# Small tables in two pools: where weights and activations start in SBUF

## The chip, the cores and the metric

The kernel runs on one core of a Trainium2 chip. The metric is the device time of one execution in microseconds (us), the median of three runs. A profile of one execution shows each engine: PE is the matrix engine (TensorE), PEld its weight loads, DVE the vector engine, ACT the scalar engine, POOL is GpSimd, SP the engine that issues most DMAs. SBUF is the on-chip memory: 128 partitions, in each of which a tile has the same byte address.

## The reference

A decoder trunk of two layers over 512 tokens of width 1024, in float32. Each layer has three steps, each followed by a residual sum and a layer norm:

```python
x = layer_norm(ALPHA * x + 0.5 * swiglu_ffn(x, ffn1_w_gu[l], ffn1_w_down[l]), ...)
x = layer_norm(ALPHA * x + hybrid_mixer(x, w_in[l], w_out[l], ...), ...)
x = layer_norm(ALPHA * x + 0.5 * swiglu_ffn(x, ffn2_w_gu[l], ffn2_w_down[l]), ...)

def swiglu_ffn(x, w_gu, w_down):
    a, u = jnp.split(x @ w_gu, 2, axis=-1)      # 1024 -> 2 * 2816
    return (jax.nn.silu(a) * u) @ w_down        # 2816 -> 1024
```

The mixer projects x once, runs windowed attention with sinks on half of the columns and retention with decay on the other half, normalises the retention per head, gates it, and projects back. Most of the work is the matrix products of the four feed-forward steps.

## The kernel before

**Products in three parts.** A float32 operand is split into a high part (rounded to fp32r) and a low part (the rest): `split` (L168 on ACT, L169 on DVE). `mm3` (L183 to L185) then issues three matmuls for each product: high by high, and the two mixed ones. A matmul has 128 columns of weights (the stationary operand, loaded just before by a weight load) and a moving operand of 256 or 512 columns, and adds into PSUM (`ps`). In the profile's names `ps<-xh,uh` the first after the arrow is the moving operand and the second the weights. Every matmul has a weight load of its own; the load for the next matmul starts as the current matmul starts.

**Units and raws.** Weights come from HBM by DMA into `raw` (two tiles of 8 KB a partition), and are split into a *unit*: a pair `uh`, `ul` of 128 x 1024 (4 KB a partition each). There are six such pairs (`UBUFS`). A unit holds eight blocks of 128 columns, 512 bytes each, or two blocks of 512 columns. `Weights` (L47 and below) hands the units out in a fixed order and starts the split of a new one when one is given back (`W.done`).

**The activations** lie transposed in `xh` and `xl` (128 x 8 x 512 each).

**One feed-forward step** (`ffn`). It goes through the gate and up columns in 11 groups of 256 columns. Groups 2 to 10 (`SEVEN`) use `glu7`, seven half-size products in place of eight: some multiply units by blocks of `xh`, `xl` (`xb`), the others by sums of such blocks held in `Th`, `Tl` (`tb`), all 256 columns wide. Groups 0 and 1 are plain (`glu`), 256 or 512 columns wide. The down projection (`seventh`, `down`) turns the operands round: activations, written block by block into `xh`, `xl` by `operand`, are the weights, and units are the moving operand, 512 columns wide. Its weight sums are made by DMAs on POOL's queue that add into `R` (L389). A few products of each down projection use other weights: `early` (a unit that holds activations) and `room` (`hr`).

**The mixer** multiplies units by `xh` (feature-major) and `xh` by units (token-major, `proj_tok`), both 512 or 256 wide. The output projection (`half`) uses `ya` with weights in the 4 KB tiles `b` of pool `mix`, then `xh` with units.

**Small tables.** `mhalf` is a constant of -0.5 for a power on POOL. Pool `small` holds statistics of the layer norm (`st`, `mv`, `ve`, `rs`), of the attention (`den`, `m`, `es`) and of the retention (`gmu`, `gvar`), three buffers each. `sk` and `nsk` hold the sinks.

**Where tiles lie.** Pools are laid out one behind the other in the order in which they are opened, and a tile takes its bytes rounded up to 32. 2,176 bytes (2,048 of DMA scratch and four constants of 32) come first. So in the kernel before:

| pool | what | bytes a partition | start of its main tiles, modulo 512 |
|---|---|---|---|
| base | `ident` 512, `mhalf` 32, `xh`, `xl`, `Y` 16,384 each | 49,696 | `ident` 128; `xh`, `xl`, `Y` 160 |
| rawp | 2 x 8,192 | 16,384 | `raw` 160 |
| unit | 12 x 4,096 | 49,152 | `uh`, `ul` 160 |
| small | `st` 3 x 64, eight others 3 x 32 | 960 | |
| ffn pools | `hT` 45,056, `S`, `Th`, `Tl` and others | | `hT`, `S`, `Th`, `Tl`, `R`, `hr` 96 |
| mixer pools | tables 6,144 with `rsc` 128 and `sk`, `nsk` 32 each beside them, then the rest | | `qk`, `rr`, `va`, `b`, `ya`, `vr` 288 |

The tables of the mixer's first row are `ropeC`, `ropeS`, `band`, `causal` and `diag`. The pools of a step start where `small` ends, and take one another's place from step to step.

Of the kernel before, what the change touches and what calls it, by code (L numbers as in the profile page):

```python
# [7 lines left out]
F32 = mybir.dt.float32  # L8
# [10 lines left out]
P = 128  # L19
# [27 lines left out]
class Weights:  # L47


    def __init__(self, T, items):  # L50
        self.T, self.items = T, items
        self.emitted = self.taken = self.out = 0
        self.ready = []
        self.raws = {}
        self.last = {raw: i for i, (raw, _, _, _) in enumerate(items)}
# [44 lines left out]
class Trunk:  # L100
    def __init__(self, tc, ctx):
        self.tc, self.nc = tc, tc.nc
        self.n = 0
        self.now = 0
        self.pin = True
        self.tasks = []
        self.later = []
        self.pace = None
        self.halves = 2
        nc = self.nc  # L110
        self.base = ctx.enter_context(tc.tile_pool(name="base", bufs=1))
        self.rawp = ctx.enter_context(tc.tile_pool(name="rawp", bufs=2))
        self.unit = ctx.enter_context(tc.tile_pool(name="unit", bufs=UBUFS))
        self.small = ctx.enter_context(tc.tile_pool(name="small", bufs=3))
        self.psum = ctx.enter_context(tc.tile_pool(name="psum", bufs=8, space=PSUM))
        self.ident = self.base.tile([P, P], F32, name="ident")
        make_identity(nc, self.ident)
        self.mhalf = self.base.tile([P, 8], F32, name="mhalf")
        nc.vector.memset(self.mhalf, -0.5)
        self.xh = self.base.tile([P, KC, SEQ], F32R, name="xh")  # L120
        self.xl = self.base.tile([P, KC, SEQ], F32R, name="xl")
        self.Y = self.base.tile([P, NT, D], F32, name="Y")
# [370 lines left out]
    def norm(self, t, halves, gb, out=None, delay=4, scale=(ALPHA, ALPHA)):  # L493
        nc = self.nc
        g, b = gb
        y = self.Y[:, t, :]
        st = self.small.tile([P, 2, 6], F32, tag="st", name=self.nm("st"))
        for h in range(2):
            hs = slice(h * 512, (h + 1) * 512)
            nc.vector.scalar_tensor_tensor(out=y[:, hs], in0=y[:, hs], scalar=scale[h], in1=halves[h],  # L500
                                           op0=ALU.mult, op1=ALU.add)
            nc.vector.bn_stats(out=st[:, h, :], in_=y[:, hs])
        mv = self.small.tile([P, 2], F32, tag="mv", name=self.nm("mv"))
        nc.vector.bn_aggr(out=mv, in_=st)
        ve = self.small.tile([P, 1], F32, tag="ve", name=self.nm("ve"))
        nc.vector.tensor_scalar_add(ve, mv[:, 1:2], LN_EPS)
        rs = self.small.tile([P, 1], F32, tag="rs", name=self.nm("rs"))
        nc.gpsimd.tensor_tensor(out=rs, in0=ve, in1=self.mhalf[:, 0:1], op=ALU.pow)
        nc.vector.scalar_tensor_tensor(out=y, in0=y, scalar=mv[:, 0:1], in1=g, op0=ALU.subtract, op1=ALU.mult)
        parts = [slice(0, D)] if out is None else [slice(0, 512), slice(512, D)]  # L510
        for hs in parts:
            nc.vector.scalar_tensor_tensor(out=y[:, hs], in0=y[:, hs], scalar=rs, in1=b[:, hs],
                                           op0=ALU.mult, op1=ALU.add)
            if out is not None:
                nc.sync.dma_start(out[t * P : (t + 1) * P, hs], y[:, hs])
        if out is None:
            self.pend.append(self.spawn(self.y_to_xT(t), delay))
# [293 lines left out]
    def mixer(self, sinks, cst, g, b):  # L811
        nc, tc, W = self.nc, self.tc, self.W
        with ExitStack() as ctx:
            cp = self.cpool = ctx.enter_context(tc.tile_pool(name=self.nm("mixc"), bufs=1))
            pool = self.mpool = ctx.enter_context(tc.tile_pool(name=self.nm("mix"), bufs=1))
            self.c = {}
            c = self.c

            def const(name, tag=None):
                ap = cst[name]  # L820
                c[name] = cp.tile(list(ap.shape), F32, tag=tag or name, name=self.nm(name))
                nc.sync.dma_start(c[name], ap)
# [2 lines left out]
            const("ropeS", "sin")  # L825
            for name in ("band", "causal", "diag", "rsc"):
                const(name)
            sk = c["sk"] = cp.tile([P, 8], F32, name=self.nm("sk"))
            nc.sync.dma_start(sk, sinks.partition_broadcast(P))
            c["nsk"] = cp.tile([P, 8], F32, name=self.nm("nsk"))  # L830
            nc.vector.tensor_scalar_mul(c["nsk"], sk, -1.0)

            self.kT = [self.tmp("qk", 6, F32R) for _ in range(2)]
# [128 lines left out]
    def attention(self, n):  # L962


        nc = self.nc
        c = self.c
        k0 = max(n - 1, 0) * P
        nk = (n + 1) * P - k0
        nb = nk // P
        ns = slice(n * P, (n + 1) * P)  # L970
        mm = nc.tensor.matmul
        s = [self.big([P, 4, 2 * P]) for _ in range(2)]
        for c2 in range(2):
            sb = [self.ps().rearrange("p (c k) -> p c k", c=2) for _ in range(2)]
            q, k = self.qT[c2], self.kT
            for cc in range(2):
                for i, (qi, ki) in enumerate(((0, 0), (0, 1), (1, 0))):
                    for kv in range(2):
                        pr = slice(kv * HD, (kv + 1) * HD)
                        mm(sb[kv][:, cc, :nk], q[qi][pr, cc, ns], k[ki][pr, k0 : k0 + nk], start=i == 0, stop=i == 2)  # L980
            for kv in range(2):
                nc.vector.tensor_tensor(out=s[kv][:, c2 * 2 : c2 * 2 + 2, :nk], in0=sb[kv][:, :, :nk],
                                        in1=c["band"][:, None, 2 * P - nk :].to_broadcast([P, 2, nk]), op=ALU.min)
        for kv in range(2):
            hs = slice(kv * 4, kv * 4 + 4)
            den = self.small.tile([P, 4], F32, tag="den", name=self.nm("den"))
            m = self.small.tile([P, 4], F32, tag="m", name=self.nm("m"))
            nc.vector.tensor_reduce(out=m, in_=s[kv][:, :, :nk], op=ALU.max, axis=AX.X)
            nc.vector.scalar_tensor_tensor(out=m, in0=m, scalar=-SCALE, in1=c["nsk"][:, hs], op0=ALU.mult, op1=ALU.min)
            es = self.small.tile([P, 4], F32, tag="es", name=self.nm("es"))  # L990
            nc.vector.tensor_add(es, m, c["sk"][:, hs])
            for cc in range(4):
                nc.scalar.activation(s[kv][:, cc, :nk], s[kv][:, cc, :nk], AF.Exp, bias=m[:, cc : cc + 1], scale=SCALE,
                                     accum_out=den[:, cc : cc + 1])
            nc.scalar.activation(es, es, AF.Exp)
            nc.vector.tensor_add(den, den, es)
            nc.vector.reciprocal(den, den)
            for cc in range(4):
                nc.scalar.activation(s[kv][:, cc, :nk], s[kv][:, cc, :nk], AF.Copy, scale=den[:, cc : cc + 1])
            yield 3  # L1000
        pT = []
        for kv in range(2):
            pT.append(self.big([P, 2, 512]))
            for kb in range(nb):
                tb = self.ps()
                for cc in range(4):
                    nc.tensor.transpose(tb[:, cc * P : (cc + 1) * P], s[kv][:, cc, kb * P : (kb + 1) * P], self.ident)  # L1007
                nc.scalar.copy(pT[kv][:, kb, :], tb)
            yield 1 + kv
        yb = self.ps()  # L1010
        for kb in range(nb):
            blk = n - nb + 1 + kb
            for kv in range(2):
                cs = slice(kv * HD, (kv + 1) * HD)
                mm(yb[cs, :], self.va[:, blk, cs], pT[kv][:, kb, :], start=kb == 0, stop=kb == nb - 1)  # L1015
        self.split(self.ya[0][:, :, ns], self.ya[1][:, :, ns], yb.rearrange("p (c q) -> p c q", c=4))

    def retention(self, p, qT, kT):
        nc = self.nc
        c, vr, O = self.c, self.vr, self.O  # L1020
# [9 lines left out]
        for h, sb in enumerate(banks):  # L1030
            st = self.tmp("rr", 10).rearrange("p (n i) -> p n i", n=NT)
# [19 lines left out]
        st = self.tmp("rr", 10)[:, :N3].rearrange("p (n e) -> p n e", n=NT - 1)  # L1051
# [19 lines left out]
        G = 2 * NT  # L1071
# [1 line left out]
        nc.vector.tensor_tensor(out=oc, in0=ob.rearrange("p (n h e) -> p n h e", n=NT, h=2),  # L1073
                                in1=wq[:, None, hp, None].to_broadcast([P, NT, 2, HD]), op=ALU.mult)
        ocg = oc.rearrange("p n h e -> p (n h) e")
        mu = self.small.tile([P, G], F32, tag="gmu", name=self.nm("gmu"))
        nc.vector.tensor_reduce(out=mu, in_=ocg, op=ALU.add, axis=AX.X)
        nc.vector.tensor_scalar_mul(mu, mu, 1.0 / HD)
        nc.vector.tensor_tensor(out=ocg, in0=ocg, in1=mu[:, :, None].to_broadcast([P, G, HD]), op=ALU.subtract)
# [108 lines left out]
```

## Time and profile before

| | |
|---|---|
| median of three runs | 1766.73 us (1766.64 to 1767.32) |
| span of the profiled execution | 1765.1 us, 1.6 us under the median |
| granted TensorE clock, mean | 0.998 of full speed |
| ACT casts L168 `uh<-S`, 128 x 1024 | 144, mean 1049 ns |
| DVE subtractions L169 `ul<-S,uh`, 128 x 1024 | 144, mean 1222 ns |
| DMA | 216.34 MB, mean 123 GB/s |

Busy time is the time in which at least one instruction of an engine runs, so two matmuls in flight count once. In the groups of instructions, the two numbers behind the count are the busy time in us and the mean duration of one in ns, and behind the second bar stands the idle time before them with what ended it. In the timeline, the first number is the start of an instruction in us from the start of the span, the second its duration. In the table of stretches, each engine has its busy time and, in brackets, the number of instructions, and the row ends with the granted clock, the busy share of the DMA engines and GB/s. In the view of waits a row has the total, the number and the longest.

### The profile page before, as it was taken

The numbers are of one execution on the slowest core, as the hardware profiler recorded it, in microseconds if no ns is written. First come the engines' busy times: TensorE is split into PE (matmuls) and PEld (weight loads), VectorE is DVE, ScalarE is ACT, GpSimd is POOL, SyncE is SP. The second block draws the span as 40 slices with busy tenths as digits, with TensorE's granted clock in tenths as the row PEclk, the third lists the DMA queues.
The fourth block names the chain that finished last, engine by engine and source line by source line (L and its number), as shares of the span: only waits on it lengthen the run. The fifth ranks groups of instructions, "written<-read, shape, count | busy, mean of one in ns | idle before, by whom it ended". The sixth has DMA issues, their size and how long they took to land.

```text
span 1765.1 us, 29166 instructions
## 1 busy us (share of the span) xinstructions
PE 1752.7 (99%) x11930; PEld 1600.5 (91%) x11930; DVE 1414.9 (80%) x1975; ACT 928.1 (53%) x1456; POOL 182.9 (10%) x152
## 2 busy tenths in 40 slices
PE   9999999999999999999999999999999999999998
PEld 9999988887789999998899999889877899999886
DVE  7888888856767888878888888888567587888887
ACT  5455556378712455555535555554795234555561
POOL 0000022111111000014000000311011110000131
PEclk9999999999999999999999999999999999999999
DMA  6234389422222243369423334982233122334891
GB/s 191 97 96 133 131 202 199 131 85 88 73 79 72 74 137 102 97 208 214 140 68 99 121 96 147 211 203 91 85 95 96 48 95 97 97 96 132 211 218 48
DMA packets 163765, 216.34 MB, mean 123 GB/s; under 512 B 5168, under 2 KB 116528, under 8 KB 163632
## 3 DMA queue, kind: packets, MB, share of 16 engines
q1 hardware_dynamic: 141872, 172.55, 30.5%
q0 software_dynamic: 21760, 41.95, 13.1%
q8 instruction: 93, 1.52, 0.3%
q14 instruction: 40, 0.33, 0.1%
HBM read 212.38 MB, written 2.10 MB: 122 GB/s over the span
## 4 chain that ended last, share of the span: by engine, by line
PE 90%; issue 6%; DMA 1%; DVE 1%; POOL 1%; ACT 0%; SPq 0%; POOLq 0%; DVEq 0%
PE ps L183 29%; PE ps L185 29%; PE ps L184 29%; PE ps L476 1%; DMA raw<-in_ffn_w_gu_dram 1%; POOL sw L959 1%; PE ps L1067 1%; PE ps L1015 0%; PE ps L1029 0%; PE ps L1063 0%; PE ps L1050 0%; DMA retS<-c_retS_dram 0%; ACT sw L957 0%; DVE ul L169 0%; PE ps L1007 0%
## 5 line engine op out<-in xcount | busy, mean ns | idle before, releaser
L183 PE MATMUL ps<-xh,uh 128*128 128x256 f32 (+1 forms) x1616 | 482.2, 298 | 0.0
L185 PE MATMUL ps<-xh,ul 128*128 128x256 f32 (+1 forms) x1616 | 479.3, 297 | 1.0 <-DVE ul L169 0.9
L184 PE MATMUL ps<-xl,uh 128*128 128x256 f32 (+1 forms) x1616 | 478.5, 296 | 0.3 <-DVE xl L169 0.3
L168 ACT CAST uh<-raw 128x1024 fp32r<-128x1024 f32 (+1 forms) x274 | 237.1, 886 | 245.6 <-PE ps L184 140.1
L169 DVE TENSOR_TENSOR ul<-raw,uh 128x1024 fp32r<-128x1024 f32 (+1 forms) x274 | 273.3, 1013 | 62.2 <-ACT uh L168 61.6
L183 PE MATMUL ps<-Th,uh 128*128 128x256 f32 x1152 | 319.1, 277 | 0.0
L184 PE MATMUL ps<-Tl,uh 128*128 128x256 f32 x1152 | 318.7, 277 | 0.0
L185 PE MATMUL ps<-Th,ul 128*128 128x256 f32 x1152 | 318.3, 276 | 0.0
L185 PEld LDWEIGHTS ps<-xh,ul 128*128 128x128 f32 x1616 | 307.9, 191 | 10.1 <-DVE ul L169 1.6
L183 PEld LDWEIGHTS ps<-xh,uh 128*128 128x128 f32 x1616 | 307.9, 191 | 9.7 <-issue 1.6
L184 PEld LDWEIGHTS ps<-xl,uh 128*128 128x128 f32 x1616 | 308.0, 191 | 7.9 <-DVE xl L169 0.5
L183 PE MATMUL ps<-uh,xh 128*128 128x512 f32 x720 | 283.4, 394 | 0.5 <-ACT xh L168 0.5
L185 PE MATMUL ps<-uh,xl 128*128 128x512 f32 x720 | 280.8, 390 | 0.0
L184 PE MATMUL ps<-ul,xh 128*128 128x512 f32 x720 | 280.3, 389 | 0.0
L168 ACT CAST uh<-S 128x1024 fp32r<-128x1024 f32 x144 | 151.1, 1049 | 149.0 <-PE ps L184 145.2
L169 DVE TENSOR_TENSOR ul<-S,uh 128x1024 fp32r<-128x1024 f32 x144 | 175.9, 1222 | 60.1 <-ACT uh L168 59.5
L184 PEld LDWEIGHTS ps<-Tl,uh 128*128 128x128 f32 x1152 | 216.7, 188 | 0.0
L183 PEld LDWEIGHTS ps<-Th,uh 128*128 128x128 f32 x1152 | 216.6, 188 | 0.0
L185 PEld LDWEIGHTS ps<-Th,ul 128*128 128x128 f32 x1152 | 216.4, 188 | 0.0
L389 POOL DMA_DIRECT2D R<-in_ffn_w_down_dram x80 | 97.1, 1217 | 1020.7 <-DVE ul L169 930.0
L169 DVE TENSOR_TENSOR ul<-R,uh 128x1024 fp32r<-128x1024 f32 x120 | 145.1, 1221 | 25.8 <-ACT uh L168 25.7
L183 PEld LDWEIGHTS ps<-uh,xh 128*128 128x128 f32 x720 | 135.2, 188 | 30.1 <-issue 1.6
(143 smaller groups left out, 2362.4 us busy)
## 6 DMA issues: line engine op xcount, KB each, us to landing
raw<-in_ffn_w_gu_dram SPq DMA_DIRECT2D x86, 1024.0 KB, 5.5
R<-in_ffn_w_down_dram POOLq DMA_DIRECT2D x80, 512.0 KB, 7.6
raw<-in_w_in_dram SPq DMA_DIRECT2D x18, 1024.0 KB, 5.2
R<-in_ffn_w_down_dram SPq DMA_DIRECT2D x16, 1024.0 KB, 6.3
raw<-in_ffn_w_down_dram SPq DMA_DIRECT2D x12, 1024.0 KB, 7.2
R<-in_ffn_w_down_dram SPq DMA_DIRECT2D x8, 512.0 KB, 4.3
raw<-in_w_in_dram SPq DMA_DIRECT2D x8, 512.0 KB, 6.1
raw<-in_w_out_dram SPq DMA_DIRECT2D x8, 512.0 KB, 6.4
```

The lines of the kernel that those rows point to most:

```text
L168: a = self.nc.scalar.copy(hi, src)
L169: b = self.low = self.nc.vector.tensor_sub(lo, src, hi.bitcast(F32))
L183: keep(mm(out, ah, bh, start=start, stop=False, **kw))
L184: keep(mm(out, ah, bl, start=False, stop=False, **kw))
L185: keep(mm(out, al, bh, start=False, stop=stop, **kw))
L389: self.nc.gpsimd.dma_start(src, rows(i, j, g * 2, 2), accum_op=ALU.add))
L476: nc.tensor.transpose(b[:, c * P : (c + 1) * P], src[:, c * P : (c + 1) * P], self.ident)
L959: nc.gpsimd.tensor_mul(sw[:, :n], sw[:, :n], S)
L1067: ins = nc.tensor.matmul(ob[:, o0 : o0 + HD], ST[h][:, n, :], vr[:, n, p * P + h * HD : p * P + (h + 1) * HD], start=n == 0, stop=n == 0 o ...
```

## The change

`mhalf` leaves pool `base` and goes, 16 columns wide, into a new pool `near` that is opened between `rawp` and `unit`. The tables `st`, `den`, `m`, `es` and `gmu` move from `small` to `near`, with three buffers as before. `mv`, `ve`, `rs` and `gvar` stay in `small`. `sk` and `nsk` get 16 columns, of which the first 8 are used. What is computed does not change, nor does the order of the work as it is written, but for the memset of `mhalf`, which now stands before the making of `ident`.

```diff
         self.rawp = ctx.enter_context(tc.tile_pool(name="rawp", bufs=2))
+        self.near = ctx.enter_context(tc.tile_pool(name="near", bufs=3))
+        self.mhalf = self.near.tile([P, 16], F32, tag="mhalf", name="mhalf", bufs=1)
+        nc.vector.memset(self.mhalf, -0.5)
         self.unit = ctx.enter_context(tc.tile_pool(name="unit", bufs=UBUFS))
         self.small = ctx.enter_context(tc.tile_pool(name="small", bufs=3))
...
-        self.mhalf = self.base.tile([P, 8], F32, name="mhalf")
-        nc.vector.memset(self.mhalf, -0.5)
...
-        st = self.small.tile([P, 2, 6], F32, tag="st", name=self.nm("st"))
+        st = self.near.tile([P, 2, 6], F32, tag="st", name=self.nm("st"))
...
-            sk = c["sk"] = cp.tile([P, 8], F32, name=self.nm("sk"))
+            sk = c["sk"] = cp.tile([P, 16], F32, name=self.nm("sk"))[:, :8]
...
-            c["nsk"] = cp.tile([P, 8], F32, name=self.nm("nsk"))
+            c["nsk"] = cp.tile([P, 16], F32, name=self.nm("nsk"))[:, :8]
...
-            den = self.small.tile([P, 4], F32, tag="den", name=self.nm("den"))
-            m = self.small.tile([P, 4], F32, tag="m", name=self.nm("m"))
+            den = self.near.tile([P, 4], F32, tag="den", name=self.nm("den"))
+            m = self.near.tile([P, 4], F32, tag="m", name=self.nm("m"))
...
-            es = self.small.tile([P, 4], F32, tag="es", name=self.nm("es"))
+            es = self.near.tile([P, 4], F32, tag="es", name=self.nm("es"))
...
-        mu = self.small.tile([P, G], F32, tag="gmu", name=self.nm("gmu"))
+        mu = self.near.tile([P, G], F32, tag="gmu", name=self.nm("gmu"))
```

## The prediction

> **What bounds the kernel now.** I read the page's first part, then the chain that ended last, then the waits of PE.
>
> ```profile
> span 1765.1 us, 29166 instructions
> PE 1752.7 (99%) x11930; PEld 1600.5 (91%) x11930; DVE 1414.9 (80%) x1975; ACT 928.1 (53%) x1456; POOL 182.9 (10%) x152
> PE 90%; issue 6%; DMA 1%; DVE 1%; POOL 1%; ACT 0%; SPq 0%; POOLq 0%; DVEq 0%
> ```
> ```profile
> PE ps L468 <- POOL ident masks.py:199: 1.4, 1, 1.4
> PE ps L185 <- DVE ul L169: 0.9, 2, 0.7
> PE ps L1029 <- DVE rr L1032: 0.8, 2, 0.4
> ```
> The matrix engine is busy 99% of the span and its longest waits for others come to some 3 us. So the time is the number of matmuls times the pace at which one follows another. Only something that changes that pace moves the time, and all of such a change counts until a producer is late.
>
> The mean duration of a matmul is not its pace, because two are in flight at once. The pace is read from start times. First, products of xh with units, 256 columns wide: 48 of them, from 57.37 to the start of the first product with Th.
>
> ```profile
> 57.37 0.28 PE L183 MATMUL ps<-xh,uh 128*128 128x256 f32 x1
> ...
> 63.00 0.28 PE L185 MATMUL ps<-xh,ul 128*128 128x256 f32 x1
> 63.12 0.29 PE L183 MATMUL ps<-Th,uh 128*128 128x256 f32 x1
> ```
> That is 5.75 us / 48 = 119.8 ns. Next the 60 products with Th from 63.12, of the same shape and with the same kind of unit as weights, up to the next product with xh (the last of the 60 and that one):
>
> ```profile
> 69.82 0.28 PE L185 MATMUL ps<-Th,ul 128*128 128x256 f32 x1
> 69.94 0.28 PE L183 MATMUL ps<-xh,uh 128*128 128x256 f32 x1
> ```
> 6.82 us / 60 = 113.7 ns. Then 179 starts of the 512-column products in the down projection:
>
> ```profile
> 249.62 0.39 PE L184 MATMUL ps<-ul,xh 128*128 128x512 f32 x1
> ...
> 289.96 0.39 PE L185 MATMUL ps<-uh,xl 128*128 128x512 f32 x1
> ```
> 40.34 us / 178 = 226.6 ns. The difference between 512 and 256 columns, 226.6 - 119.8 = 106.8 ns, is the streaming of 256 columns. What is left over is an **overhead per matmul**: 13.0 ns for xh at either width, 6.9 ns for Th.
>
> Why should Th be cheaper? By the layout given with the kernel, units and xh both start 160 bytes past a multiple of 512, and Th 96 past one. Every block of weights is 128 columns = 512 bytes and every moving block 1024 or 2048, so these remainders hold for all blocks. **Distance 0 costs 13.0 ns, distance 64 costs 6.9 ns.** The weight loads say the same, being a little longer with xh:
>
> ```profile
> L183 PEld LDWEIGHTS ps<-xh,uh 128*128 128x128 f32 x1616 | 307.9, 191 | 9.7 <-issue 1.6
> L183 PEld LDWEIGHTS ps<-Th,uh 128*128 128x128 f32 x1152 | 216.6, 188 | 0.0
> ```
> I take it that the load of the next weights and the running stream read SBUF at once, and hinder each other when they start at the same remainder. That is inferred from two distances, not shown.
>
> **The change part by part.** The instructions, their number, their buffers and their DMAs stay. Two tables per layer get 32 bytes wider; SyncE issues the same loads. The memset of mhalf takes 16 columns instead of 8:
>
> ```profile
> L119 DVE MEMSET mhalf<- 128x8 f32 x1 | 0.1, 65 | 0.8 <-PEq L1174 0.8
> ```
> 65 ns at the start, under the wait of 1.4 us for ident: nothing.
>
> What changes are remainders. Without mhalf in base, xh, xl, Y and raw go from 160 to 128. The pool near holds 64 + 192 + 3*96 + 96 = 640 bytes, so units start at (128 + 640) mod 512 = 256. Pool small holds 4*96 = 384, so hT and Th start at (256 + 384) mod 512 = 128. In the mixer 128 + 128 + 64 + 64 = 384 for ya and the t4k tiles, both alike as before. So the distance from activation to unit becomes 128, for xh and for Th. Where the unit is the moving operand and xh the weights (down products, token-major projections), it is -128. Counts:
>
> ```profile
> L183 PE MATMUL ps<-xh,uh 128*128 128x256 f32 x1408 | 398.5, 283 | 0.0
> L183 PE MATMUL ps<-Th,uh 128*128 128x256 f32 x1152 | 319.1, 277 | 0.0
> L183 PE MATMUL ps<-uh,xh 128*128 128x512 f32 x720 | 283.4, 394 | 0.5 <-ACT xh L168 0.5
> L183 PE MATMUL ps<-xh,uh 128*128 128x512 f32 x208 | 83.6, 402 | 0.0
> ```
> Each stands for three (L183 to L185): 4224 with xh at 256 columns, 3456 with Th, and 3 * (720 + 208) = 2784 at 512. The 480 with hr, yah or another unit as weights keep distance 0.
>
> No row shows distance 128. One end: it helps no more than 64 does, 6.9 ns. The other is the least overhead in the trace, 16 transposes in 1.91 us:
>
> ```profile
> 895.84 1.91 PE L476 MATMUL ps<-ident,Y 128*128 128x128 f32 x16
> L476 PE MATMUL ps<-ident,Y 128*128 128x128 f32 x192 | 25.2, 276 | 0.3 <-DMA Y<-in_x_dram 0.3
> ```
> (1.91 - 0.28) / 15 = 108.7 to 109.3 ns by rounding; I use 109.3, so 2.5 ns over 106.8. A straight line through 13.0 and 6.9 would be below that at 128. I take the middle, **4.7 ns**, for both signs:
> - xh, 256 columns: (13.0 - 4.7) * 4224 = 35.1 us
> - Th: (6.9 - 4.7) * 3456 = 7.6 us
> - 512 columns: (13.0 - 4.7) * 2784 = 23.1 us
>
> Together 65.8 us. With 6.9 ns it is 25.8 + 0 + 17.0 = 42.8 us; with 2.5 ns 44.4 + 15.2 + 29.2 = 88.8 us.
>
> The Trainium skill, "TensorE: Matmul & The Clock Gate", section "Back-to-back issue gap", gives N/2.4 + 2.5 ns for matmuls in a row, so 109.2 and 215.8 ns here. No product of this trace reaches that; by it the sum would be the 88.8 us end.
>
> **What it costs.** Transposes of Y have ident 32 bytes away now and 0 after: at most the 6.1 ns between Th and xh on 192 of them, 1.2 us; I take 0.5. Then the cover: does a faster PE catch up with its producers?
>
> ```profile
> 82.60:102.20 19.60, 19.60 (x171) 19.60 (x170) 16.98 (x27) 10.62 (x16) 0.00 (x0) 1.00 0.33 108
> 233.10:314.70 81.60, 81.60 (x363) 67.55 (x362) 70.99 (x70) 47.06 (x49) 24.39 (x20) 1.00 0.99 219
> ```
> ```profile
> ACT uh L168 <- PE ps L184: 294.9, 263, 4.2
> DVE ul L169 <- ACT uh L168: 148.9, 181, 4.7
> ACT uh L168 <- DMA R<-in_ffn_w_down_dram: 37.7, 35, 2.4
> ```
> One group of gate products takes 19.6 us, with 16.98 us of DVE. Even the full gain of 10% there leaves DVE some slack, and ACT mostly waits for PE to give units back, not the other way round. The down projection is tighter: in its 81.6 us DVE works 71.0 and the DMA engines are full, and ACT already waits for R. There 360 products would save 8.3 ns each, 3.0 us of 81.6. Six units lie ready ahead, 12 matmuls of 226.6 ns each, so 2.7 us a unit; that swallows 3 us. If it didn't, the four stages would give back 12 us at most. I take 2 us lost, mixer included, where chains of DVE, ACT and POOL are short of cover.
>
> 65.8 - 0.5 - 2 = 63.3 us. The profiled execution is 1765.1 us of span, 1.6 under the median of 1766.7; that rest stays. **1766.7 - 63.3 = 1703.4, said as 1704 us.**
>
> **The rivals.**
> 1. Nothing beyond Th's pace: any distance but 0 costs 6.9 ns. For it: a weight load reads 512 bytes while the stream reads 1024, so the one may overtake the other once wherever they start. 42.8 - 2.5 = 40.3 us, 1726.
> 2. The hindrance goes altogether, 2.5 ns left: 88.8 - 4 = 85 us, 1682; producers cost more then.
> 3. The sign counts: -128 does nothing for the 512-column products. All of those with a distance that I can see are at 0, so nothing speaks against it. 35.1 + 7.6 - 2.5 = 40 us, 1727; with Th's pace for xh only 25.8 us, 1741.
> 4. **Slower**: what counts is the distance modulo 128, not 512. Then 128 is as bad as 0, xh gains nothing, and Th, which has 64 by chance, loses it: 3456 * 6.1 = 21.1 us, 1788. It decides as soon as the other 7008 products gain under 21.1 / 7008 = 3.0 ns each. Neither 0 nor 64 tells a period of 128 from one of 512.
> 5. Nothing happens: xh and Th differ by where they lie (xh ahead of the units, Th behind them), or the remainders are not what I worked out. 1766.7. Against it: the 13.0 ns is the same at both widths and with either operand as weights.
>
> The Trainium skill has a rule for the fifth: in "TensorE: Matmul & The Clock Gate", section "Step-by-step: what each phase is for", "Loading the next tile's weights doesn't steal SBUF read bandwidth from the running matmul". By that rule start addresses cannot matter. The trace does not agree as it stands: 119.8 against 113.7 ns for one shape, so it gets little.
>
> **How the numbers follow.** Forecast, overhead between 3.5 and 6 ns: 0.34. Rival 1: 0.20, rival 2: 0.18, rival 3: 0.14, rival 4: 0.09, rival 5: 0.05. Faster by over 0.2% (3.5 us, about what a measurement of this kernel can tell): 0.86; same 0.05; slower 0.09. The range takes the forecast and rivals 1 to 3, from 1676 (rival 2 with nothing lost is 1678) to 1742; rivals 4 and 5 stay out.
>
> **What would show it.** Right: 48 products with xh at under 5.5 us instead of 5.75; their weight loads at 188 ns or less instead of 191; the mean duration of a 512-column product with xh below 394 ns; PE still at 99%. The step on distance 128 is wrong if xh keeps 119.8 or Th slows to it; the step on signs if 512 columns stay at 226.6; the cover if PE's waits for ACT uh or DVE ul grow beyond 5 us. A product with hr or yah should keep 227; if it changes as well, remainders are not the reason.

## The result: slower by 1.5%, and the profile after

The changed kernel takes 1793.99 us (median of 4 runs, 1793.76 to 1794.6), the kernel before on the same chip 1767.03 us (4 runs, 1766.64 to 1767.98). The ratio is 1.0153, with a 95% interval of 1.0138 to 1.0167: 27.0 us slower, where 63 us of gain were forecast.

The first part of the page of the changed kernel, and the first line of its chain that ended last:

```profile
span 1792.1 us, 29166 instructions
...
PE 1779.8 (99%) x11930; PEld 1615.1 (90%) x11930; DVE 1417.3 (79%) x1975; ACT 928.0 (52%) x1456; POOL 181.7 (10%) x152
...
PE 97%; DMA 1%; DVE 1%; ACT 0%; SPq 0%; POOLq 0%; issue 0%; DVEq 0%; ACTq 0%
```

Its longest waits of PE (total us, times, longest):

```profile
PE ps L469 <- POOL ident masks.py:199: 1.4, 1, 1.4
PE ps L186 <- DVE ul L170: 1.0, 2, 0.8
```

The same number of instructions, the same engine at 99%, no new wait. The span grew by 27.0 us and PE's busy time by 27.1 us. So the matmuls themselves follow one another more slowly. The groups of instructions, with shapes kept apart (lines moved by one; busy us and mean ns behind the count):

```profile
L184 PE MATMUL ps<-xh,uh 128*128 128x256 f32 x1408 | 397.1, 282 | 0.2 <-ACT uh L169 0.2
...
L184 PE MATMUL ps<-Th,uh 128*128 128x256 f32 x1152 | 324.2, 281 | 0.0
...
L184 PEld LDWEIGHTS ps<-xh,uh 128*128 128x128 f32 x1616 | 304.3, 188 | 10.8 <-issue 1.6 <-ACT uh L169 0.4
...
L184 PE MATMUL ps<-uh,xh 128*128 128x512 f32 x720 | 286.8, 398 | 0.5 <-ACT xh L169 0.5
```

Against the rows of before, a product with Th went from 277 to 281 ns, a 512-column product with units from 394 to 398, one with xh from 283 to 282. The weight loads with xh fell from 191 to 188 ns, as the prediction hoped, and brought little. Paces come from starts again. In the timeline of the changed kernel, 48 products with xh begin at 57.84, 60 with Th at 63.53; 336 products of the down projection begin at 242.70, and 24 with `hr` at 320.78:

```profile
57.84 0.28 PE L184 MATMUL ps<-xh,uh 128*128 128x256 f32 x1
...
63.53 0.28 PE L184 MATMUL ps<-Th,uh 128*128 128x256 f32 x1
...
70.65 0.28 PE L184 MATMUL ps<-xh,uh 128*128 128x256 f32 x1
...
242.70 0.40 PE L184 MATMUL ps<-uh,xh 128*128 128x512 f32 x1
...
320.78 0.39 PE L184 MATMUL ps<-uh,hr 128*128 128x512 f32 x1
...
326.23 0.40 PE L184 MATMUL ps<-uh,xh 128*128 128x512 f32 x1
```

5.69 us / 48 = **118.5 ns** with xh (119.8 before), 7.12 / 60 = **118.7 ns** with Th (113.7 before), 78.08 / 336 = **232.4 ns** at 512 columns (226.6 before), and 5.45 / 24 = 227.1 ns with `hr`, which lies at distance 0 in both kernels, since `hr` and its units lie in one pool of the step.

The differences between one start and the next, added up over the whole trace for each kind of product, close the account. All kernels of this study that do the trunk's work stand in the table; distances are those from xh and from Th to the units, in bytes. "Units by xh" are the products with units as the moving operand and xh as weights, which takes in the down projection and the mixer's token-major products; for them the distance has the other sign:

| kernel | xh / Th | xh, 256 columns (4224) | Th (3456) | units by xh, 512 (2160) | xh, 512 (624) | rest | span, us |
|---|---|---|---|---|---|---|---|
| before | 0 / 64 | 508.0 | 393.7 | 495.1 | 145.6 | 212.8 | 1765.1 |
| after | 128 / 128 | 505.3 | 410.1 | 506.4 | 148.2 | 212.2 | 1792.1 |
| T64 | 128 / 64 | 505.6 | 394.6 | 506.1 | 148.2 | 211.7 | 1776.1 |
| T128only | 0 / 128 | 509.3 | 410.5 | 495.2 | 145.7 | 213.4 | 1784.0 |
| all64 | 64 / 64 | 487.7 | 391.7 | 499.2 | 148.6 | 213.2 | 1750.3 |
| views | 64 (down 0) / 64 | 490.8 | 395.5 | 496.6 | 148.6 | 212.4 | 1753.9 |
| all76 | 76 / 76 | 510.2 | 414.7 | 508.1 | 151.5 | 211.0 | 1805.5 |

After against before: -2.7 with xh, +16.4 with Th, +11.3 and +2.6 at 512 columns, -0.6 in the rest, together +27.0 us.

### The profile page after: what moved, and what is told of

Same layout as the page of the kernel before. It is cut to its first block, busy times and chain, and to the rows that moved or that the text cites. A ratio compares the mean times of both kernels' runs of the same rounds, so it can differ in the third digit from the quotient of the medians.

```text
span 1792.1 us, 29166 instructions
## 1 busy us (share of the span) xinstructions
PE 1779.8 (99%) x11930; PEld 1615.1 (90%) x11930; DVE 1417.3 (79%) x1975; ACT 928.0 (52%) x1456; POOL 181.7 (10%) x152
## 4 chain that ended last, share of the span: by engine, by line
PE 97%; DMA 1%; DVE 1%; ACT 0%; SPq 0%; POOLq 0%; issue 0%; DVEq 0%; ACTq 0%
PE ps L184 31%; PE ps L186 30%; PE ps L185 30%; DMA raw<-in_ffn_w_gu_dram 1%; PE ps L477 1%; PE ps L1016 1%; PE ps L981 1%; PE ps L1068 1%; PE ps L1008 1%; PE ps L1030 1%; DVE ul L170 0%; PE ps L1064 0%; PE ps L1051 0%; PE ps L1041 0%; ACT uh L169 0%; DVE xl L170 0%
## 5 line engine op out<-in xcount | busy, mean ns | idle before, releaser
L185 PE MATMUL ps<-Tl,uh 128*128 128x256 f32 x1152 | 324.2, 281 | 0.0
L184 PE MATMUL ps<-Th,uh 128*128 128x256 f32 x1152 | 324.2, 281 | 0.0
L186 PE MATMUL ps<-Th,ul 128*128 128x256 f32 x1152 | 324.2, 281 | 0.0
L184 PEld LDWEIGHTS ps<-xh,uh 128*128 128x128 f32 x1616 | 304.3, 188 | 10.8 <-issue 1.6
L186 PEld LDWEIGHTS ps<-xh,ul 128*128 128x128 f32 x1616 | 304.2, 188 | 10.9 <-DVE ul L170 1.7
L185 PEld LDWEIGHTS ps<-xl,uh 128*128 128x128 f32 x1616 | 304.3, 188 | 8.8 <-DVE xl L170 0.5
L186 PE MATMUL ps<-uh,xl 128*128 128x512 f32 x720 | 284.4, 395 | 0.0
L185 PE MATMUL ps<-ul,xh 128*128 128x512 f32 x720 | 284.0, 394 | 0.0
```

The costliest lines, as they stand in the source:

```text
L184: keep(mm(out, ah, bh, start=start, stop=False, **kw))
L185: keep(mm(out, ah, bl, start=False, stop=False, **kw))
L186: keep(mm(out, al, bh, start=False, stop=stop, **kw))
```

## The experiments

**1. The curve itself (sweep).** Matmuls alone, of 256 and of 512 columns, with the weights in one tile and the moving operand in another, at every distance from 0 to 496 bytes in steps of 16. Distance is the start of the weights minus the start of the moving operand.

```diff
+        def block(tag, width, mo, d, count, stride=512):
+            ps = psum.tile([P, 512], F32, tag="b%d" % (n[0] % 8), name=tag)
...
+            for k in range(count):
+                m0 = mo // 4 + k % 4 * 512
+                w0 = mo // 4 + d // 4 + k % 8 * (stride // 4)
+                keep(nc.tensor.matmul(ps[:, :width], W[:, w0 : w0 + P], M[:, m0 : m0 + width],
+                                      start=k == 0, stop=k == count - 1))
...
+        for d in range(0, 512, 16):
+            block("n256d%dx" % d, 256, 0, d, 60)
+            block("n512d%dx" % d, 512, 0, d, 36)
```

> This kernel does none of the trunk's work; it only issues matmuls with real data: for each distance from the moving operand to the weights (0 to 496 bytes modulo 512 in steps of 16) 60 matmuls of 256 columns and 36 of 512, and four distances again with both operands moved by 32 and by 96 bytes. Theory A, the distance modulo 512 sets the pace: 256 columns at 119 to 120 ns for distance 0, 113 for 64, 118 to 119 for 128, the same after both operands are moved; 512 columns 227 at 0 and 232 at 384 (which is -128). Theory B, what counts is where the operands start by themselves (in the changed kernel all starts are multiples of 128, in the kernel before all were 32 past a multiple of 64): the pace hardly depends on the distance and differs between the blocks moved by 0, 32 and 96 bytes. Theory C, modulo 128: the same pace at 0, 128, 256 and 384, and 113 at 64, 192, 320 and 448.

The groups of this run; the name gives columns and distance, behind the count stands the busy time of the whole block:

```profile
L37 PE MATMUL n512d128x<-M,W 128*128 128x512 f32 x36 | 8.6, 395 | 0.0
...
L37 PE MATMUL n512d0x<-M,W 128*128 128x512 f32 x36 | 8.3, 390 | 0.0
...
L37 PE MATMUL n256d0x<-M,W 128*128 128x256 f32 x60 | 7.4, 283 | 0.0
...
L37 PE MATMUL n256d128x<-M,W 128*128 128x256 f32 x60 | 7.3, 281 | 0.0
L37 PE MATMUL n256d384x<-M,W 128*128 128x256 f32 x60 | 7.3, 281 | 0.0
...
L37 PE MATMUL n256d64x<-M,W 128*128 128x256 f32 x60 | 7.0, 276 | 0.0
L37 PE MATMUL n256d320x<-M,W 128*128 128x256 f32 x60 | 7.0, 276 | 0.0
```

Of 60 products a block at 64 takes 7.0 us, at 0 and at 128 it takes 7.4 and 7.3; at 512 columns 0 is the cheaper one. From the starts of each block, without its first eight, in ns:

| distance | 0 | 16 | 32 | 48 | 64 | 80 | 96 | 112 |
|---|---|---|---|---|---|---|---|---|
| 256 columns | 120.00 | 118.24 | 118.37 | 117.78 | **113.33** | 118.65 | 118.69 | 119.98 |
| 512 columns | **226.67** | 233.41 | 233.37 | 233.30 | 233.22 | 232.00 | 234.41 | 233.33 |

| distance | 128 | 144 | 160 | 176 | 192 | 208 | 224 | 240 |
|---|---|---|---|---|---|---|---|---|
| 256 columns | 118.59 | 120.00 | 119.96 | 118.06 | 117.78 | 116.65 | 116.67 | 117.39 |
| 512 columns | 233.48 | 233.41 | 233.33 | 230.00 | 228.89 | 233.33 | 233.33 | **226.67** |

From 256 on the row repeats: 256 gives 120.00, 320 gives 113.33, 384 gives 118.59. **The period is 256, not 512**, and the curve does not fall smoothly: at 256 columns 64 is a single dip among neighbours of 117.8 and 118.7, and at 512 columns 0 is near the best there is. No clock, producer or DMA of the trunk is needed for it: 120.00, 113.33 and 118.59 are the 119.8, 113.7 and 118.5 to 118.7 of the two kernels, 226.67 and 233.48 their 226.6 and 232.4.

Both operands begun 32 or 96 bytes later changed nothing at 0 (120.00) and little at 128 (118.73); at 64 they gave 117.8 in place of 113.33, which theory A did not have and experiment 5 takes up. So theory A stands but for its period and for 64, and theories B and C fall. Two points of this curve were measured in the kernel before; the prediction drew the rest.

The Trainium skill, "TensorE: Matmul & The Clock Gate", section "Step-by-step: what each phase is for", gives the streaming operand and the weight load read ports of their own. The prediction inferred from it that start addresses cannot matter. This run, with nothing beside the matmuls, does not agree with that: 113.33 against 120.00 ns.

**2. Th alone (T64).** The changed kernel with 64 bytes more in pool `small`, which puts the units 64 past Th again and leaves all else.

```diff
         self.small = ctx.enter_context(tc.tile_pool(name="small", bufs=3))
+        pad = self.small.tile([P, 16], F32, tag="pad", name="pad", bufs=1)
+        nc.vector.memset(pad, 0.0)
```

> The changed kernel with 64 bytes more in pool small, so that Th lies 64 bytes before units again and all else is as in the changed kernel. Theory A: Th returns from 118.7 to 113.7 ns, 3456 x 5 = 17 us, so 1777 us; xh at 119.6 and the 512-column products at 232 stay. Theory B: Th stays at 118.7 and the time at 1794. Theory C: as A.

1777.78 us (1777.49 to 1778.4), 16.2 under the changed kernel; against before the ratio is 1.0059 (1.0043 to 1.0076). In its timeline the 60 products with Th begin at 62.84 and the next with xh at 69.67:

```profile
62.84 0.28 PE L186 MATMUL ps<-Th,uh 128*128 128x256 f32 x1
...
69.67 0.28 PE L186 MATMUL ps<-xh,uh 128*128 128x256 f32 x1
```

6.83 us / 60 = 113.8 ns. So 16.2 of the 27 us are Th's lost dip. The other 10.8 are what xh at 128 costs; by the table -2.4 at 256 columns, +11.0 and +2.6 at 512.

**3. The other way round (T128only).** The kernel before with 192 bytes more in `small`: Th goes to 128, xh stays at 0.

```diff
         self.small = ctx.enter_context(tc.tile_pool(name="small", bufs=3))
+        pad = self.small.tile([P, 48], F32, tag="pad", name="pad", bufs=1)
+        nc.vector.memset(pad, 0.0)
```

> The kernel before with 192 bytes more in pool small: Th lies at 288 and units at 160, so Th is 128 bytes from units modulo 256; xh stays at distance 0. This is one part of the change alone. Theory A2: Th rises from 113.7 to about 118.7 ns, 3456 x 4.9 = 17 us, all else as before: 1784 us. Rival, the sign or the period of 512 counts (here the distance from Th to units is 384 modulo 512, not 128): a pace of Th that differs from 118.7.

1785.7 us (1785.65 to 1786.7), ratio 1.0105 (1.0092 to 1.0118). The products with Th again, 60 of them:

```profile
63.54 0.28 PE L185 MATMUL ps<-Th,uh 128*128 128x256 f32 x1
...
70.66 0.28 PE L185 MATMUL ps<-xh,uh 128*128 128x256 f32 x1
```

7.12 / 60 = 118.7 ns, as in the changed kernel. With xh at 0 the down products keep their 495.2 us. One group alone was moved; it lost 16.8 us, and no other group changed by more than 1.3.

**4. Everything at 64 (all64).** Only `mhalf` moves out of base, 64 bytes wide, behind `raw`; the tables stay in `small`. Units then lie 64 past xh and 64 past Th.

```diff
         self.rawp = ctx.enter_context(tc.tile_pool(name="rawp", bufs=2))
+        self.near = ctx.enter_context(tc.tile_pool(name="near", bufs=1))
+        self.mhalf = self.near.tile([P, 16], F32, name="mhalf")
+        nc.vector.memset(self.mhalf, -0.5)
...
-        self.mhalf = self.base.tile([P, 8], F32, name="mhalf")
-        nc.vector.memset(self.mhalf, -0.5)
```

> The kernel before with mhalf alone moved behind raw, so that units lie 64 bytes past xh and past Th, and xh 64 bytes before units where the roles are turned. Theory A: products with xh of 256 columns fall from 119.8 to about 113.7 ns, 4224 x 6.1 = 26 us gained; Th keeps 113.7; the 512-column products at -64 are open (each ns is 2.8 us). 1741 us if they keep 227. Theory B: starts are at 128 and 192, so Th rises to about 119 as in the changed kernel and the time is 1783 or more. Theory C: as A.

**1750.19 us** (1748.81 to 1752.1), ratio 0.9904 (0.9889 to 0.9918): faster than both kernels. Its timeline, with 48 products with xh, 60 with Th, 336 of the down projection, and last 72 with xh in the mixer:

```profile
57.54 0.28 PE L184 MATMUL ps<-xh,uh 128*128 128x256 f32 x1
...
62.99 0.28 PE L184 MATMUL ps<-Th,uh 128*128 128x256 f32 x1
...
69.79 0.28 PE L184 MATMUL ps<-xh,uh 128*128 128x256 f32 x1
...
234.36 0.39 PE L184 MATMUL ps<-uh,xh 128*128 128x512 f32 x1
...
311.27 0.39 PE L184 MATMUL ps<-uh,hr 128*128 128x512 f32 x1
...
337.71 0.28 PE L184 MATMUL ps<-xh,uh 128*128 128x256 f32 x1
...
346.19 0.38 PE L477 MATMUL ps<-ident,Y 128*128 128x128 f32 x2
```

5.45 / 48 = 113.5, 6.80 / 60 = 113.3, 76.91 / 336 = 228.9 (the sweep's value at -64, which is 192 modulo 256), but 8.48 / 72 = 117.8 in the mixer. The expected 1741 us were not reached: the down products lie at 228.9, not 226.7, and a part of the products with xh runs at 117.8 at the same distance. Over the trace xh gains 20.3 us at 256 columns; with 113.33 ns throughout it would be 508.0 - 4224 x 0.11333 = 29.3. But for the 1.4 us for ident, the longest waits of PE are:

```profile
PE ps L186 <- DVE ul L170: 1.0, 2, 0.8
PE ps L184 <- ACT uh L169: 0.7, 1, 0.7
```

**5. Two paces at one distance (sweep2).** In the first run 64 gave 113.33 with the operands at 0, but 117.78 with both begun 32 or 96 bytes later. Either the common start counts, or what ran before. So 64 follows five different blocks here; besides, there are steps of 4 bytes around 64, weights of 64 columns, and other widths.

```diff
+        for wide, dl in ((512, 0), (256, 0), (256, 128), (256, 192), (256, 224)):
+            block("lead%dd%dx" % (wide, dl), wide, 0, dl, 24)
+            block("d64after%dd%dx" % (wide, dl), 256, 0, 64, 120)
...
+        for d in (0, 64, 128, 192):
+            block("c64n256d%dx" % d, 256, 0, d, 60, cols=64)
+            block("c64n512d%dx" % d, 512, 0, d, 36, cols=64)
```

> Again matmuls alone, none of the trunk's work. Theory A2: the pace is a function of the distance modulo 256, with one narrow dip at 64 for 256 columns, and there are two steady ways of running at 64 (113.3 and 117.8 ns); which one is taken depends on the matmuls just before. Then 56 to 72 differ from 113.3 by steps, 48 and 80 stand at 117.8 and 118.7 as in the first sweep; at 64 the pace is 113.3 after 512-column matmuls and 117.8 after 256-column ones at distance 0, for every common start (0, 32, 64, 96, 160). Rival: the common start decides, so 32, 96 and 160 stay at 117.8 after the same lead. With 64 columns of weights a load reads half as long: if load and stream hinder each other, the overhead of 512 columns shrinks by half or more (under 220 ns at distance 0); if the overhead belongs to the stream alone it stays at 227. One block repeats the same weights and the same moving columns at distance 64: 113.3 if only starts count.

The groups of this run; "after" names the block before:

```profile
L40 PE MATMUL d64after256d0x<-M,W 128*128 128x256 f32 x120 | 14.3, 281 | 0.0
L40 PE MATMUL d64after256d128x<-M,W 128*128 128x256 f32 x120 | 14.3, 281 | 0.0
L40 PE MATMUL d64after512d0x<-M,W 128*128 128x256 f32 x120 | 14.3, 281 | 0.0
...
L40 PE MATMUL d64after256d192x<-M,W 128*128 128x256 f32 x120 | 13.8, 276 | 0.0
L40 PE MATMUL d64after256d224x<-M,W 128*128 128x256 f32 x120 | 13.8, 276 | 0.0
...
L40 PE MATMUL c64n512d0x<-M,W 128*64 128x512 f32 x36 | 8.4, 392 | 0.0
...
L40 PE MATMUL c64n256d0x<-M,W 128*64 128x256 f32 x60 | 7.0, 276 | 0.0
...
L40 PEld LDWEIGHTS c64n512d0x<-M,W 128*64 128x64 f32 x36 | 4.8, 134 | 3.3
```

The same 120 products, the same addresses: 14.3 or 13.8 us, 117.77 or 113.33 ns by their starts, held to the end of the block. **The distance 64 has two steady paces, and what ran before can choose.** The guess that a lead of 512 columns brings the quick pace fell: common starts of 32, 64, 96 and 160 after 512 columns with the same start all gave 117.78, and so did a block that repeats the same weights and moving columns. The starts of the block have a say as well: in experiment 8, after the same 12 products of 512 columns, 64 gave 117.78 at common start 0 and 113.33 at 16 and 32. What the rule is stays open. The two paces in all64 are these two; what ran before them was not varied there.

Of the steps around 64, 76 gave 113.33 and the other eight 117.8 to 120.0, 64 itself among them. Weights of 64 columns load in 134 ns instead of 188, but the product of 512 columns at distance 0 then came every 229.63 ns, not sooner than 226.67. At 256 columns and distance 0, though, it came every 113.33 ns in place of 120.00, and at 512 columns and distance 128 every 229.19 in place of 233.48. At distance 0 products of 320 and 384 columns came every 146.67 and 173.33 ns, so 64 columns stream in 26.67 ns and 256 in 106.7 (448 columns came every 202.56 ns, not quite on that line).

**6. A second view for the down products (views).** all64, with a second view of xh and xl that starts 64 bytes later for the operands of the down projection, to bring those back to distance 0. Small tables fill the gaps between the tiles, so other addresses of these tables change too. The late operands overwrite 16 columns of the activations that the next step reads, so part of its input is changed.

```diff
+        def two(name):
+            t = self.base.tile([P, KC * SEQ + 16], F32R, name=name)
+            return [t[:, o : o + KC * SEQ].rearrange("p (k s) -> p k s", k=KC) for o in (0, 16)]
...
-                hh, hl = (v[:, k : k + f, h * 256 : (h + 1) * 256] for v in (self.xh, self.xl))
+                hh, hl = (v[:, k : k + f, h * 256 : (h + 1) * 256] for v in (self.oh, self.ol))
```

> The kernel before with units 64 bytes past xh and Th, as in the run with 64 everywhere, and with a second view of xh and xl that starts 64 bytes later, into which the down projection writes its operands, so that these lie at distance 0 from units again. st and gvar lie in base for that. Theory A2: 256-column products at 113.3 ns (117.8 in some stretches), down products at 226.7 instead of 228.9 to 230, 1584 x 2.7 = 4 us under the run with 64 everywhere: 1746 us. Rival: the views overlap by 16 columns, so transposed activations of the next step have to wait for the last operands; if that is on the path the 4 us are lost and the time is 1750 or more.

1756.7 us (median of six), ratio 0.9935 (0.9911 to 0.9959); 1746 us were expected. Five executions lie between 1747.38 and 1763.1 us, wider apart than what the run was to show, and one took 5058.45 us, for which no reason is known. The 336 down products in its timeline:

```profile
232.79 0.39 PE L196 MATMUL ps<-uh,xh 128*128 128x512 f32 x1
...
308.95 0.39 PE L196 MATMUL ps<-uh,hr 128*128 128x512 f32 x1
```

76.16 / 336 = 226.7 ns, as expected, 2.6 us less over the trace than in all64. But xh and Th at 256 columns took 3.1 and 3.8 us more at an unchanged distance of 64. By starts it is the second pace: of the 72 stretches of 24 or 60 products with Th, all run at 113.3 ns in all64, while 18 (756 products) run at 117.8 here, which makes 756 x 4.45 ns = 3.4 us of the 3.8. PE waits no longer than 1.4 us for anything, so the wait that the rival named is not seen. Which pace a stretch gets can't be told from the distances alone.

**7. A distance with one pace? (all76).** In the fine steps 76 gave 113.33 where 64 did not. So xh, xl, Th and Tl begin some columns into wider tiles, with units 76 past all of them modulo 256.

```diff
-        self.xh = self.base.tile([P, KC, SEQ], F32R, name="xh")
...
+        self.xh = self.shifted(self.base, "xh", 8, 5)
...
+    def shifted(self, pool, name, more, off, dims=(KC, SEQ)):
+        t = pool.tile([P, KC * SEQ + more], F32R, name=name)
+        t = t[:, off : off + KC * SEQ]
...
-            Th = gp.tile([P, 4, H, 256], F32R, name=self.nm("Th"))
+            Th = self.shifted(gp, self.nm("Th"), 64, 45, (4, H, 256))
```

> The kernel before, with xh, xl, Th and Tl begun some columns into wider tiles and the units placed so that they lie 76 bytes past all four modulo 256 (64 in the run all64). In the matmuls run alone 76 gave 113.33 ns at 256 columns, like 64, but in the one stretch where it was tried. Theory A (pace is set by the distance of the starts modulo 256, and 76 has one steady way): all products with xh and Th of 256 columns at 113.3 ns; against all64, where those with xh came to 115.5 on average, 4224 x 2.2 ns = 9.3 us less. The 512-column products with xh as weights lie at -76, so 180 modulo 256; 176 gave 230.0 and 192 gave 228.9, so up to 2160 x 1.1 = 2.4 us more. Together 1750.2 - 9.3 + 0 to 2.4 = 1741 to 1743 us. Rival (76 has two ways as 64 has, the other near its neighbours' 118.4): xh 4224 x 2.9 and Th 3456 x 5.1 ns more than in all64, 1750 + 12 + 18 = 1780; a mixture lies between.

1807.59 us (1807.1 to 1807.9), ratio 1.023 (1.0216 to 1.0244): the slowest of all. Its 60 products with Th:

```profile
63.51 0.28 PE L198 MATMUL ps<-Th,uh 128*128 128x256 f32 x1
...
70.71 0.28 PE L198 MATMUL ps<-xh,uh 128*128 128x256 f32 x1
```

7.20 / 60 = 120.0 ns, worse than either theory had it. The kernel differs from the fine steps in more than the distance: there the moving operand began at 0 modulo 256, here at 148, which is no multiple of 32.

**8. The moving operand's own start (sweep3).** Distances 0, 64, 76 and 128 with both operands begun 0 to 32 and 148 bytes past a multiple of 256.

```diff
+        for mo in (0, 4, 8, 12, 16, 20, 24, 28, 32, 148):
+            for d in (0, 64, 76, 128):
+                block("leadx", 512, 0, 0, 12)
+                block("m%dd%dx" % (mo, d), 256, mo, d, 60)
```

> Matmuls alone, without the work of the trunk: 256 columns at distances 0, 64, 76 and 128, with both operands begun 0 to 32 and 148 bytes past a multiple of 256, each block after 12 products of 512 columns at distance 0; then 76 after other products; then 512 columns. It asks why the run all76 was slow, where the products of 256 columns came every 117 and 123 ns in turn, 120 on average. Theory D (the distance alone counts, and 76 has two steady ways, as 64 has): with both begun at 148 and after 12 products of 512 columns distance 76 gives 113.33 as at 0; after products of 256 columns at other distances some blocks of 76 give 117 to 120. Theory E (the moving operand's own start counts when it is no multiple of 32 bytes): 113.33 at common starts 0 and 32, about 120 at 20 and 148, for 64 and 76 alike; after other products 76 keeps 113.33. Distance 0 should give 120.00 at 0 and 32 by both.

The groups of this run; m is the common start, d the distance:

```profile
L40 PE MATMUL n512m20d0x<-M,W 128*128 128x512 f32 x48 | 11.6, 400 | 0.0
...
L40 PE MATMUL n512m0d0x<-M,W 128*128 128x512 f32 x48 | 11.1, 389 | 0.0
...
L40 PE MATMUL m148d76x<-M,W 128*128 128x256 f32 x60 | 7.4, 283 | 0.0
...
L40 PE MATMUL m32d76x<-M,W 128*128 128x256 f32 x60 | 7.4, 283 | 0.0
...
L40 PE MATMUL m20d76x<-M,W 128*128 128x256 f32 x60 | 7.4, 283 | 0.0
...
L40 PE MATMUL m0d64x<-M,W 128*128 128x256 f32 x60 | 7.2, 281 | 0.0
...
L40 PE MATMUL m32d64x<-M,W 128*128 128x256 f32 x60 | 7.0, 277 | 0.0
...
L40 PE MATMUL m0d76x<-M,W 128*128 128x256 f32 x60 | 7.0, 276 | 0.0
```

By starts, 76 gave 113.33 at common start 0, also after products of 256 columns at distances 0, 64, 128 and 192; and 120.00 at 32, 120.06 at 20, 120.08 at 148. At 20 and 148, the 512-column products came every 236.7 to 239.2 ns at all three distances tried, 0 among them. Distance 0 went from 226.67 to 238.31 there, so a start 20 bytes past a multiple of 32 (148 is one too) costs by itself, and theory D (distance alone) falls. Not every start off the multiples of 32 does: at 256 columns and distance 0, common starts of 16 and 28 came every 116.7 ns, sooner than the 120.00 at 0 and 32. Theory E is right for 20 and 148, and wrong for 32, where 76 was slow as well. all76's span is 55.2 us above that of all64, and the table puts 45.5 of them on 256 columns and 11.8 on 512 (the rest is 2.2 less). With xh and Th moving, from 148, its paces are those of this run: 120.0 ns at 256 columns, and some 238 at 512 (239.2 here). Its 336 down products, whose moving units begin at 224, a multiple of 32, came every 233.33 ns, as they do here at distance 180 from common start 0.

Units at 76 with activations at a common start like 0 were not tried in the kernel: every unit would have to begin 12 bytes into a wider tile.

## Why the prediction was wrong

- **What bounds the kernel: right.** PE at 99% in every kernel here, and the sums of start differences account for all 27.0 us.
- **Paces from starts, and 106.8 ns for 256 columns: right.** Widths in sweep2 give 106.7. The overheads at 0 and 64 were 13.3 and 6.7 in the sweep, 13.0 and 6.9 in the prediction (at the slower pace of 64 it is 11.1).
- **Remainders, distances, counts: right.** T64 and T128only moved Th by a padding of 64 and 192 bytes and the products with Th answered by 15.5 and 16.8 us, no other group by more than 1.3; `hr` kept its 227 ns.
- **The failed step: the price at distance 128**, put at 4.7 ns of overhead, the middle of 6.9 and 2.5. Measured at 256 columns: 118.6 - 106.7 = 11.9 ns. At 512 columns: 232.4 - 213.4 = 19.0 ns, above the 13.0 of distance 0. Both ends were too low. The upper one took it that 128 costs no more than 64, for which no row spoke: two points can't tell a slope from a dip, and 64 is a dip. The lower one took the streaming of 256 columns off the pace of the transposes, whose row has 128 columns; nothing here shows that those stream as long, so 2.5 ns is no overhead that this trace shows. The prediction's own sign of this failure, Th slowing towards 119.8, came with 118.7. That distance 0 might be a good place, as it is for 512 columns, was in no case. The three terms, forecast and measured: xh at 256 columns 35.1 us of gain, 2.7; Th 7.6 of gain, 16.4 of loss; 512 columns 23.1 of gain, 13.9 of loss.
- **One overhead for both widths: wrong off distance 0.** 13.3 at either width at distance 0, but 11.9 and 20.1 at 128 in the sweep, 6.7 and 19.9 at 64.
- **The reason given, a load and a stream that hinder each other at the same remainder: not borne out.** It was marked as inferred. By it equal remainders should be worst, and at 512 columns they are among the best. With weights of half the columns, whose load takes 134 ns instead of 188, a product of 512 columns at distance 0 came no sooner, where by this reason the overhead should have halved. But at 256 columns and distance 0 the overhead did halve, from 13.3 to 6.7 ns, so a part of the load in it is not ruled out. What in the chip makes the steps is still open.
- **The shorter weight load as a sign of a better pace: wrong.** It fell to 188 ns as asked, and the pace at 512 columns got worse. In the sweep the load takes 188 ns at distance 144 too, where the pace is 120.00.
- **The cover: right as far as it was tried.** all64 took 17 us out of the time, and no wait of PE for `ul` or `uh` came to more than 1.0 us in all. But its gain lies in the products of 256 columns. The down projection, which the prediction called the tighter stage, was quicker than before in none of these kernels, so its cover and the 2 us put on it were not tested.
- **The rivals.** Rival 4 (a period of 128 bytes) had 1788 us and so the sign and nearly the size, but not the reason: with a period of 128 bytes the 512-column products would have kept their pace at distance 128, and they hold 13.9 of the 27 us (226.67 and 233.48 ns in the sweep). Of it one half stands: Th had 64 "by chance" and lost it, priced at 21.1 us, measured 16.4. Rival 3's separate price for the sign fell: 128 and -128 are the same modulo 256. Rivals 1, 2 and 5 fell: not every distance but 0 has Th's price, no hindrance went away, and xh ahead of the units takes Th's 113.3 ns when it lies at Th's distance (all64).

The Trainium skill ("TensorE: Matmul & The Clock Gate", section "Back-to-back issue gap") has N/2.4 + 2.5 ns, and calls it there the gap of a single, isolated matmul. No product of 256 or 512 columns here reached the 109.2 and 215.8 ns worked out from it: the quickest steady paces were 113.33 and 226.67.

## What to carry to other kernels

Two measured points give no curve: where an effect has been seen at two places only, the price at a third may lie above both or below both. A sweep of matmuls alone (here 585 us of chip time) would have shown the loss before the layout was changed. It must have the starts of the kernel, though: the 113.33 ns of distance 76 held for common start 0 and became 120 in all76. For these fp32r products, ask for each pair of operands how far their starts are apart modulo 256, and begin the moving operand on a multiple of 32: 20 bytes past one cost 11.6 ns a product at 512 columns, and other starts were not all tried. Where one tile serves two widths, 256 and 512 columns want different distances, so weigh them by their counts: all64 gives up 7.1 us at 512 columns and gains 22.3 at 256.

## What the runs showed of the hardware that was not expected

- The pace depends on the distance between the starts of weights and moving operand with a period of 256 bytes: 113.33 to 120.00 ns at 256 columns, 226.67 to 234.41 at 512.
- Several steady paces are multiples of 6.67 ns: 113.33, 120.00, 226.67, 233.33. Others, 117.78 and 228.89, are not. At some distances, as at 128, differences from start to start vary from 115 to 122 ns.
- The same products at distance 64 hold 113.33 or 117.78 ns for 120 in a row, by what ran before; in the kernel most stretches keep one of the two. Distance 128 gave 118.59 in one run and 120.00 in another.
- A common start of 20 bytes past a multiple of 32 takes the 512-column product at distance 0 from 226.67 to 238.31 ns.
- Half the columns of weights, a load of 134 ns in place of 188, take the 256-column product at distance 0 from 120.00 to 113.33 ns, and the 512-column one from 226.67 to 229.63.
